# A four-layer backbone with mixtures of experts: experts' rows added to their tokens' sums in DRAM, where they were written apart and gathered twice

## The chip, the cores and the metric

The kernel runs on one core of a Trainium2 chip. The metric is the time of one execution in microseconds on the device, as the median of several runs. A core has five engines with a queue of instructions each, which they take in order: PE multiplies matrices (PEld loads its weights), DVE and ACT do elementwise work, POOL does elementwise work and issues the indirect transfers, SP issues most loads. The transfers of all queues run on the same 16 DMA engines of the core. An engine that needs another's result waits for a semaphore, and what stands behind it in its queue waits with it.

## The reference

Four layers work on 256 latent and 256 context tokens of 1024 values. Each applies a token mixer (attention, Mamba-2, mLSTM, latent attention) and then a mixture of 16 experts, of which every token uses two, with weights:

```python
xs = xs + g1x * yx
...
def hier_moe(h, w_rg, b_rg, w_re, b_re, w_gate, w_up, w_down):
    ...
    combine = jnp.sum(jax.nn.one_hot(eid, MOE_EXPERTS, dtype=jnp.float32) * w[..., None], axis=-2)
    out = jnp.zeros_like(h)
    for e in range(MOE_EXPERTS):
        act = jax.nn.silu(h @ w_gate[e]) * (h @ w_up[e])
        out = out + combine[..., e:e + 1] * (act @ w_down[e])
    return out
```

The experts' sum is multiplied by a gate (g2) and added to the stream x. In layers 0 to 2 this is done for all 512 tokens (four tiles of 128), in layer 3 for the 256 latent ones.

## The kernel before, in words

The program is written as a list of operations, and a scheduler sets their order on every engine once, when the program is built; a change in one place can so move instructions in others. Semaphores keep what depends on each other in order. A transfer's semaphore is one of eight that the transfers of a kind (those of SP and ACT together, those of POOL) take in turn, and a transfer that takes a semaphore again waits until the one before on it has landed.

`setup` makes constants. `layers` starts with eight loads of `w_mod` and the four tiles of x, whose first norms run on ACT (L287, `xn`).

In a layer's mixture, `route` makes for each expert a list of 128 slots (`gi`, one token's number per slot; empty slots have a number that is out of bounds). Behind it `slots_of` makes the row numbers `ri` by which the results will be found, and the slots' weights (`sw`). With 512 tokens, two experts each and 16 experts, half of the 2048 slots hold a token.

`experts` goes over the 16 experts. `gather` (L748, POOL) fetches an expert's rows from DRAM into one of four tiles `xg`; it skips the empty slots. PE transposes them (L761) and multiplies with the gate and up weights, each weight split into a high and a low half (`ehi` by ACT L742, `elo` by DVE L743). `down` multiplies with the third weight, and `rows` (L795 on DVE, L796 on ACT) writes the result, times the slots' weights, into one of three tiles `y`. `keep` (L800) then writes the tile, 512 KB, to the expert's own 128 rows of `yd` in DRAM. PE does the work of one expert's gate and up beside the down of the one before. SP loads weights into a ring of tiles (`wl`, `w`) that is four experts long. Expert 15 isn't written: its part goes to the tokens by matmuls with a selection matrix (`selT`).

`combine` runs between two layers. POOL issues eight indirect gathers (L931): four fetch each token's first row of `yd` into a tile w, and four add its second row to it on the way (`compute_op=add`). For each tile PE adds expert 15's part and this sum in PSUM (L942, L943, L946), DVE multiplies with g2 (L947) and adds to x (L952, a part of it on POOL L950). The next layer's norm follows tile by tile.

Of the kernel before, what the change touches and what calls it, by code (L numbers as in the profile page):

```python
# [7 lines left out]
F32 = mybir.dt.float32  # L8
F32R = mybir.dt.float32r
BF = mybir.dt.bfloat16  # L10
I32 = mybir.dt.int32
# [6 lines left out]
D = 1024  # L18
# [5 lines left out]
class Trunk:  # L24
# [8 lines left out]
    def setup(self):  # L33
# [52 lines left out]
        for c, pat, base, cm in ((0, [[0, 4], [0, 2]], 0, 1), (1, [[128, 4], [0, 2]], -4096, 0)):  # L86
# [3 lines left out]
        self.unit = self.const.tile([128, 16], F32, name="unit")  # L90
        nc.gpsimd.iota(self.unit, pattern=[[128, 16]], base=0, channel_multiplier=0,
                       allow_small_or_imprecise_dtypes=True)

# [338 lines left out]
    def route(self, pool, small, i, tiles, C, dense=False):  # L432
# [181 lines left out]
        with self.tc.issue_after(listed.ins):  # L614
            self.slots_of(S, a12, pk, ps, T, oh, weights, count)
        self.hd = hd

    def slots_of(self, S, a12, pk, ps, T, oh, weights, count):

        nc = self.nc  # L620

        nc.vector.tensor_mul(pk, a12, self.unit.unsqueeze(1).unsqueeze(1).to_broadcast([128, T, 2, 16]))
        rw = S("rw", [T * 2])
        nc.vector.tensor_reduce(rw, pk.rearrange("p t k e -> p (t k) e"), axis=AX.X, op=OP.add)
        nc.vector.tensor_add(rw, rw, ps)
        nc.vector.tensor_scalar(rw, rw, 128.0 * 15, None, op0=OP.min)
        self.ri = self.const.tile([128, 8], I32, name="ri")[:, :T * 2]
        nc.vector.tensor_copy(self.ri, rw)
# [99 lines left out]

    def experts(self, pool, i, tiles, yd, release):
# [5 lines left out]

        nc.gpsimd.dma_start(yd[15 * self.C:, :], xgs[-1][0:1, :])
# [62 lines left out]
        def keep(e, y, eng):  # L799
            return eng.dma_start(yd[e * 128:(e + 1) * 128, :], y)  # L800
# [5 lines left out]
        for e in range(15):  # L806
# [3 lines left out]
            if y:  # L810
                keep(e - 2, y, nc.gpsimd)
# [13 lines left out]
        keep(13, y, nc.gpsimd)  # L825
        y = rows(14, down(*late))
        keep(14, y, nc.scalar)
# [89 lines left out]
    def combine(self, pool, sT, yh, yl, yd, tiles):  # L917
# [3 lines left out]
        ys, end, first = {}, self.last_mm, None  # L921

        for ti, k in self.o["go"]:
            if not k and ti % 2 == 0:
                w = self.H.tile([128, 2048], F32, name="w", bufs=self.o["ring"])
                ys[ti], ys[ti + 1] = w[:, :D], w[:, D:]
            dst, add = ys[ti], dict(compute_op=OP.add) if k else {}
            if k and not ti and self.o["y0"]:
                dst, add = pool.tile([128, D], F32, name="y0"), {}
                first = dst  # L930
            last = nc.gpsimd.indirect_dma_start(  # L931
                out=dst, out_offset=None, in_=yd,
# [1125 lines left out]
```

## Time and profile before

| | |
|---|---|
| median of three runs | 2178.94 us (2167.51 to 2183.6) |
| profiled execution | 2178.66 us |
| its span | 2176.9 us, 30735 instructions |
| PE busy | 1935.9 us (89%) |
| DVE, ACT, POOL busy | 1493.3, 1037.2, 597.7 us |
| DMA | 467.22 MB, mean 215 GB/s |

Busy time counts the time in which an engine works. What it waits for stands in the lists of waits and in the chain that ended last, which goes back from the last instruction to what released each. The first layer's experts run from about 320 to 490 us, the second's and third's in the same way around 1080 and 1620 us. A row of the timeline has the start and the length in us, the engine, the line, out<-in, and in brackets how long the engine sat idle before and what ended that. "DMA to landing" is the time from an issue to the semaphore that says that all data has arrived, where the trace shows somebody who waits for it.

### The profile page before, as it was taken

How to read it: one execution, taken by the hardware profiler on the slowest of the kernel's cores; microseconds unless marked ns; L12 is line 12 of the kernel's file. 1: busy time of each engine (PE TensorE's matmuls, PEld its weight loads, DVE VectorE, ACT ScalarE, POOL GpSimd, SP SyncE). 2: the span in 40 equal slices, each digit the busy share in tenths (PEclk: the TensorE clock that was granted, in tenths of full speed). 3: DMA queues.
4: the chain of work that ended last, by engine and by line, in shares of the span. 5: the costliest groups of instructions: out<-in, count | busy, mean ns of one | idle time of the engine just before them, and what ended most of it. 6: DMA issues, size and time to landing. Idle time of an engine off the chain costs nothing.

```text
span 2176.9 us, 30735 instructions
## 1 busy us (share of the span) xinstructions
PE 1935.9 (89%) x11044; PEld 1440.9 (66%) x11044; DVE 1493.3 (69%) x2892; ACT 1037.2 (48%) x2054; POOL 597.7 (27%) x546
## 2 busy tenths in 40 slices
PE   5989979997988899896699969997879988998996
PEld 2965677765666676665577646886777765657542
DVE  3557567876798899888788755137768875586334
ACT  3447437764453443443377633226537764453111
POOL 2012241113564656564411121003331122001000
PEclk8989989998999999998799979999989998899998
DMA  9344758965635434444699547643649967707782
GB/s 340 134 154 158 260 178 329 396 226 154 197 111 159 139 135 142 143 162 155 222 335 397 205 130 227 223 181 117 227 175 352 406 209 235 286 15 282 280 307 101
DMA packets 176466, 467.22 MB, mean 215 GB/s; under 512 B 35065, under 2 KB 78177, under 8 KB 155824
## 3 DMA queue, kind: packets, MB, share of 16 engines
q1 hardware_dynamic: 152112, 396.01, 50.9%
q0 software_dynamic: 23488, 67.33, 9.6%
q8 instruction: 89, 1.46, 0.3%
q10 hardware_dynamic: 704, 1.82, 0.2%
q14 instruction: 73, 0.60, 0.1%
HBM read 446.44 MB, written 31.24 MB: 219 GB/s over the span
## 4 chain that ended last, share of the span: by engine, by line
PE 66%; DVE 19%; DMA 6%; ACT 3%; issue 3%; POOL 1%; SPq 0%; ACTq 0%; POOLq 0%; DVEq 0%
PE acc L201 11%; PE acc L202 11%; PE acc L203 11%; PE acc L779 3%; PE wm L225 3%; PE acc L872 3%; DVE M L1338 3%; DVE W L1344 2%; PE core L203 2%; PE core L201 2%; PE core L202 2%; PE tr L761 2%; DMA A<-acd 2%; PE tr L858 2%; PE core L1111 1%
## 5 line engine op out<-in xcount | busy, mean ns | idle before, releaser
L743 DVE TENSOR_TENSOR elo<-wl,ehi 128x1024 fp32r<-128x1024 f32 x156 | 187.1, 1220 | 22.2 <-ACT ehi L742 21.3
L742 ACT ACTIVATE ehi<-wl 128x1024 fp32r<-128x1024 f32 x156 | 161.4, 1055 | 54.3 <-PE acc L203 32.2
L748 POOL DMA_INDIRECT xg<-hd,gi x48 | 63.9, 1331 | 282.5 <-PE tr L761 227.5
L225 PE MATMUL wm<-w,cs 128*32 128x512 f32 x768 | 118.4, 634 | 20.3 <-DMA w<-in_w_mod_dram 20.2
L201 PE MATMUL acc<-hhi,wch 128*128 128x512 f32 (+1 forms) x336 | 132.7, 396 | 3.8 <-DVE zt L1311 2.7
L203 PE MATMUL acc<-split_hi,hlo 128*128 128x256 f32 x464 | 131.4, 285 | 0.2 <-DVE var L289 0.2
L202 PE MATMUL acc<-hlo,wch 128*128 128x512 f32 (+1 forms) x336 | 131.5, 392 | 0.0
L203 PE MATMUL acc<-hhi,wcl 128*128 128x512 f32 (+1 forms) x336 | 131.0, 391 | 0.0
L201 PE MATMUL acc<-split_hi,hhi 128*128 128x256 f32 x464 | 131.0, 287 | 0.0
L202 PE MATMUL acc<-split_lo,hhi 128*128 128x256 f32 x464 | 130.9, 284 | 0.0
L1263 POOL TENSOR_TENSOR wcl<-w,wch 128x512 fp32r<-128x512 f32 x76 | 109.5, 1454 | 65.9 <-ACT wch L1262 58.5
L201 PE MATMUL acc<-ehi,xTh 128*128 128x512 f32 x288 | 123.5, 429 | 2.7 <-ACT xTh L764 2.7
L202 PE MATMUL acc<-elo,xTh 128*128 128x512 f32 x288 | 118.0, 410 | 2.5 <-DVE elo L743 2.5
L203 PE MATMUL acc<-ehi,xTl 128*128 128x512 f32 x288 | 115.0, 399 | 0.0
L743 DVE TENSOR_TENSOR elo<-w,ehi 128x1024 fp32r<-128x1024 f32 x84 | 100.9, 1220 | 13.3 <-ACT ehi L742 13.3
L742 ACT ACTIVATE ehi<-w 128x1024 fp32r<-128x1024 f32 x84 | 87.0, 1052 | 27.0 <-PE acc L203 15.3
L201 PEld LDWEIGHTS acc<-split_hi,hhi 128*128 128x128 f32 x464 | 87.9, 191 | 10.2 <-issue 5.2
L376 POOL TENSOR_TENSOR x<-x,restmp 128x256 f32<-128x256 f32 (+1 forms) x46 | 48.5, 1054 | 165.4 <-DVE restmp L372 142.8
L1353 POOL TENSOR_TENSOR A<-A,CT 128x1024 f32<-128x1024 f32 x32 | 83.5, 2609 | 33.9 <-ACT A L1351 28.9
L196 DVE TENSOR_TENSOR split_lo<-w,split_hi 128x1024 fp32r<-128x1024 f32 x33 | 40.2, 1224 | 73.6 <-ACT split_hi L195 73.5
L203 PEld LDWEIGHTS acc<-split_hi,hlo 128*128 128x128 f32 x464 | 88.6, 191 | 2.7 <-DVE hhi L332 1.7
L202 PEld LDWEIGHTS acc<-split_lo,hhi 128*128 128x128 f32 x464 | 88.6, 191 | 1.5 <-issue 1.5
(613 smaller groups left out, 5674.8 us busy)
## 6 DMA issues: line engine op xcount, KB each, us to landing
w<-in_w_mod_dram SPq DMA_DIRECT2D x96, 1024.0 KB
wl<-in_moe_w_down_dram SPq DMA_DIRECT2D x47, 1024.0 KB
wl<-in_moe_w_gate_dram SPq DMA_DIRECT2D x82, 512.0 KB
wl<-in_moe_w_up_dram SPq DMA_DIRECT2D x82, 512.0 KB
w<-in_moe_w_gate_dram SPq DMA_DIRECT2D x46, 512.0 KB
w<-in_moe_w_up_dram SPq DMA_DIRECT2D x46, 512.0 KB
yd<-y POOLq DMA_DIRECT2D x42, 512.0 KB, 2.9
w<-in_ssm_w_in_dram SPq DMA_DIRECT2D x40, 512.0 KB
```

Of the source, the lines that this page charges most:

```text
L201: mm(ps, a[0], b[0], start=start, stop=False)
L202: mm(ps, a[0], b[1], start=False, stop=False)
L203: self.last_mm = mm(ps, a[1], b[0], start=False, stop=stop)
L225: nc.tensor.matmul(st["ps"][32 * g:32 * g + 32, :], self.cs[:, j, :], w[:, 512 * g:512 * g + 512], start=(j == 0), stop=(j == 7))
L742: nc.scalar.activation(hi, v, AF.Copy)
L743: nc.vector.tensor_sub(lo, v, hi)
L748: nc.gpsimd.indirect_dma_start(out=xgs[e % len(xgs)], out_offset=None, in_=self.hd, in_offset=bass.IndirectOffsetOnAxis(ap=self.gi[:, e:e ...
L779: nc.tensor.matmul(pg, x[2][:, jj, :], gu[1][:, :, 512 + 256 * jj:768 + 256 * jj], start=False, stop=(jj == 1))
L872: nc.tensor.matmul(pg[r, :], x[:, j, r], w[p][0][j // 4][:, :, j % 4 * 256:(j % 4 + 1) * 256], start=(j == 0), stop=(j == 7))
L1263: (eng or self.nc.gpsimd).tensor_sub(lo, v, hi)
L1338: nc.vector.scalar_tensor_tensor(M[:, h, c], CE[1][:, h, c], col(self.ac, 1, c, h), M[:, h, c], op0=OP.subtract, op1=OP.min)
L1353: nc.gpsimd.tensor_mul(Ah, Ah, CT.unsqueeze(1).to_broadcast([128, 2, 512]))
```

## The change

`yd` gets one row for each token (512) and 128 spare rows, and it is filled with zeros beforehand by five plain writes per layer on ACT's queue (`sums`). `keep` becomes an indirect scatter on POOL that adds the tile's rows to the rows of their tokens in DRAM (`compute_op=add`); slots without a token go to spare rows, one for each partition (`si`). `combine` loads one row per token with four plain loads on SP in place of the eight gathers on POOL. `ri` and the operations that made it go.

```diff
--- before.py
+++ after.py
@@ -87,9 +87,11 @@
             nc.gpsimd.iota(self.tokv[:, :, :, c], pattern=pat, base=base, channel_multiplier=cm,
                            allow_small_or_imprecise_dtypes=True)
 
-        self.unit = self.const.tile([128, 16], F32, name="unit")
-        nc.gpsimd.iota(self.unit, pattern=[[128, 16]], base=0, channel_multiplier=0,
+        self.spare = self.const.tile([128, 1], F32, name="spare")
+        nc.gpsimd.iota(self.spare, pattern=[[0, 1]], base=512, channel_multiplier=1,
                        allow_small_or_imprecise_dtypes=True)
+        self.zero = self.const.tile([128, 256], F32, name="zeros")
+        nc.gpsimd.memset(self.zero, 0.0)
 
         self.odd = self.const.tile([128, 8, 2], F32, name="odd")
         nc.gpsimd.iota(self.odd, pattern=[[0, 8], [64, 2]], base=0, channel_multiplier=0,
@@ -612,20 +614,15 @@
         self.gi = self.const.tile([128, 16], I32, name="gi")[:, :U]
         listed = nc.vector.tensor_copy(self.gi, xf)
         with self.tc.issue_after(listed.ins):
-            self.slots_of(S, a12, pk, ps, T, oh, weights, count)
+
+            self.si = self.const.tile([128, 16], I32, name="si")[:, :U]
+            nc.vector.tensor_scalar(self.si, xf, self.spare[:, 0:1], None, op0=OP.min)
+            self.slots_of(S, a12, ps, T, oh, weights, count)
         self.hd = hd
 
-    def slots_of(self, S, a12, pk, ps, T, oh, weights, count):
+    def slots_of(self, S, a12, ps, T, oh, weights, count):
 
         nc = self.nc
-
-        nc.vector.tensor_mul(pk, a12, self.unit.unsqueeze(1).unsqueeze(1).to_broadcast([128, T, 2, 16]))
-        rw = S("rw", [T * 2])
-        nc.vector.tensor_reduce(rw, pk.rearrange("p t k e -> p (t k) e"), axis=AX.X, op=OP.add)
-        nc.vector.tensor_add(rw, rw, ps)
-        nc.vector.tensor_scalar(rw, rw, 128.0 * 15, None, op0=OP.min)
-        self.ri = self.const.tile([128, 8], I32, name="ri")[:, :T * 2]
-        nc.vector.tensor_copy(self.ri, rw)
         weights()
         count()
 
@@ -726,14 +723,19 @@
         gu = [self.eload([v[:, h * D:(h + 1) * D] for v in (g, u)]).rearrange("p (k n) -> p k n", k=2) for h in range(2)]
         return gu, self.eload([self.I["moe_w_down"][i, e].rearrange("(p j) d -> p (j d)", j=2)])
 
+    def sums(self, i):
+
+        self.yd = self.DR.tile([5 * 128, D], F32, name=f"yd{i}")
+        for t in range(5):
+            self.nc.scalar.dma_start(self.yd[t * 128:(t + 1) * 128, :].rearrange("p (k n) -> p k n", n=256),
+                                     self.zero.unsqueeze(1).to_broadcast([128, 4, 256]))
+
     def experts(self, pool, i, tiles, yd, release):
         nc, T = self.nc, len(tiles)
         n = T * 128
         xgs = [pool.tile([128, D], F32, name=f"xg{k}") for k in range(self.o["ahead"])]
         for x in xgs:
             nc.gpsimd.memset(x, 0.0)
-
-        nc.gpsimd.dma_start(yd[15 * self.C:, :], xgs[-1][0:1, :])
 
         def chunk(v):
 
@@ -796,8 +798,11 @@
             nc.scalar.activation(y[:, 512:], py[1], AF.Copy, scale=w)
             return y
 
-        def keep(e, y, eng):
-            return eng.dma_start(yd[e * 128:(e + 1) * 128, :], y)
+        def keep(e, y):
+
+            nc.gpsimd.indirect_dma_start(
+                out=yd, out_offset=bass.IndirectOffsetOnAxis(ap=self.si[:, e:e + 1], axis=0), in_=y, in_offset=None,
+                bounds_check=n + 127, oob_is_err=True, compute_op=OP.add)
 
         for e in range(len(xgs)):
             gather(e)
@@ -808,7 +813,7 @@
             now = gate_up(e, x)
             gather(e + len(xgs))
             if y:
-                keep(e - 2, y, nc.gpsimd)
+                keep(e - 2, y)
             if late:
                 y = rows(e - 1, down(*late))
             x, late = nx, now
@@ -822,9 +827,9 @@
         sT = po.tile([128, 4, 128], F32R, name="selT")
         nc.scalar.activation(sT, pt.rearrange("p (t k) -> p t k", t=4), AF.Copy)
         sw = self.sw[:, 15:16]
-        keep(13, y, nc.gpsimd)
+        keep(13, y)
         y = rows(14, down(*late))
-        keep(14, y, nc.scalar)
+        keep(14, y)
         py = down(*gate_up(15, x))
         yh, yl = (po.tile([128, 2, 512], F32R, name="y" + k) for k in "hl")
         for nb in range(2):
@@ -918,20 +923,12 @@
 
         nc = self.nc
         g2 = self.mod_rows(pool, "g2", 2, 1)
-        ys, end, first = {}, self.last_mm, None
-
-        for ti, k in self.o["go"]:
-            if not k and ti % 2 == 0:
+        ys, end = {}, self.last_mm
+        for t in range(4):
+            if t % 2 == 0:
                 w = self.H.tile([128, 2048], F32, name="w", bufs=self.o["ring"])
-                ys[ti], ys[ti + 1] = w[:, :D], w[:, D:]
-            dst, add = ys[ti], dict(compute_op=OP.add) if k else {}
-            if k and not ti and self.o["y0"]:
-                dst, add = pool.tile([128, D], F32, name="y0"), {}
-                first = dst
-            last = nc.gpsimd.indirect_dma_start(
-                out=dst, out_offset=None, in_=yd,
-                in_offset=bass.IndirectOffsetOnAxis(ap=self.ri[:, 2 * ti + k:2 * ti + k + 1], axis=0),
-                bounds_check=yd.shape[0] - 1, oob_is_err=True, **add)
+                ys[t], ys[t + 1] = w[:, :D], w[:, D:]
+            nc.sync.dma_start(ys[t], yd[t * 128:(t + 1) * 128, :])
 
         def add(t, after=None):
             x, y, c = self.X[t], ys[t], self.o["cadd"][t]
@@ -941,13 +938,10 @@
                 with self.tc.issue_after((after or end).ins):
                     nc.tensor.matmul(ps, sT[:, t], yh[:, h], start=True, stop=False)
                 nc.tensor.matmul(ps, sT[:, t], yl[:, h], start=False, stop=False)
-                if not t and first is not None:
-                    nc.tensor.matmul(ps, self.ident, first[:, k], start=False, stop=False)
                 nc.tensor.matmul(ps, self.ident, y[:, k], start=False, stop=True)
                 nc.vector.tensor_mul(y[:, k], ps, g2[t // 2][:, k])
             if c:
-                with self.tc.issue_after(last.ins):
-                    nc.gpsimd.tensor_add(x[:, :c], x[:, :c], y[:, :c])
+                nc.gpsimd.tensor_add(x[:, :c], x[:, :c], y[:, :c])
             if c < D:
                 nc.vector.tensor_add(x[:, c:], x[:, c:], y[:, c:])
 
@@ -967,6 +961,8 @@
                 self.attn_proj(pb, w_in, kz, vr, qT)
             with self.tc.issue_after(self.last_pow.ins):
                 self.vectors()
+            if not self.dense:
+                self.sums(0)
             po = left.enter_context(self.pool("a_out"))
             with self.pool("a_soft") as pc:
                 hi, lo = self.attn_core(pc, po, kz, vr, qT)
@@ -1953,6 +1949,8 @@
                 self.fq.extend(self.mod_round(i, 1) + self.mod_round(i, 2))
                 if i < 3:
                     self.fq.extend(self.mod_round(i + 1, 0))
+                if 0 < i < 3 and not dense:
+                    self.sums(i)
                 mixers[i]()
                 if stop == f"xm{i}":
                     return self.dump()
@@ -1986,15 +1984,14 @@
                     listing.close()
                     with self.pool("moe_experts") as pool:
                         if i < 3:
-                            yd = self.DR.tile([15 * C + 1, D], F32, name=f"yd{i}")
                             last = ExitStack()
 
                             def release():
                                 keep.close()
                                 return last.enter_context(self.pool("moe_out", "right"))
 
-                            kept = self.experts(pool, i, tiles, yd, release)
-                            self.pending = self.combine(*kept, yd, tiles), last
+                            kept = self.experts(pool, i, tiles, self.yd, release)
+                            self.pending = self.combine(*kept, self.yd, tiles), last
                         else:
                             self.experts_select(pool, i, tiles)
                 picks.close()
```

The scheduler makes a new order of it. On ACT, the order at the start of the program before, the first row being the loads of a bias (`mod`) and `xn` the first norm:

```order
L49 ACTIVATE cth<-cc 128x16
L221 DMA mod_171<-in_b_mod_dram 4x512
L108 DMA vrows<-in_norm_g_dram 32x128
L221 DMA mod_1123<-in_b_mod_dram 4x512 x2
L287 ACTIVATE xn,ss<-x_69 128x1024
L287 ACTIVATE xn,ss<-x_70 128x1024
```

And now, with the three tensors `yd` of the three layers (lines are those of the changed kernel):

```order
L49 ACTIVATE cth<-cc 128x16
L223 DMA mod_173<-in_b_mod_dram 4x512
L110 DMA vrows<-in_norm_g_dram 32x128
L223 DMA mod_1125<-in_b_mod_dram 4x512 x2
L730 DMA yd_1337<-zeros 512x1x256 x5
L730 DMA yd_5224<-zeros 512x1x256 x5
L730 DMA yd_11717<-zeros 512x1x256 x5
L289 ACTIVATE xn,ss<-x_69 128x1024
L289 ACTIVATE xn,ss<-x_70 128x1024
```

All 15 fills of the three layers stand ahead of the first norm, though the diff places those of layers 1 and 2 in their layers. By the semaphores that the transfers take in turn, the eighth load of `w_mod` on SP now also waits for the ninth fill, and the first load of the attention's weights for the tenth.

On POOL, the end of the first layer's experts before, with the eight gathers of `combine` at L931 (`g` is the gate g2):

```order
L748 DMA xg_3571<-hd_3312,gi 128x1024
L800 DMA yd_3567<-y 128x1024 x5
L269 DMA g_5178<-md_2117 128x1024
L269 DMA g_5180<-md_2117 128x1024
L800 DMA yd_3567<-y 128x1024
L248 MEMSET mod_8432 64x512
L931 DMA w<-yd_3567,ri 128x1024 x8
L950 TENSOR_TENSOR x_70<-x_70,w 128x512
```

And now, where each scatter waits for a semaphore of POOL's transfers (DMASW), the one of the scatter before it among them:

```order
L750 DMA xg_3571<-hd_3320,gi 128x1024 [waits DMASW3_49,PE_49]
L803 DMA yd_1337<-y,si 640x1024 [waits DMASW0_49,DVE_49,Activation_49]
L750 DMA xg_3572<-hd_3320,gi 128x1024 [waits DMASW5_49,PE_49]
L750 DMA xg_3573<-hd_3320,gi 128x1024 [waits DMASW7_49,PE_49]
L803 DMA yd_1337<-y,si 640x1024 [waits DMASW3_49,DVE_49,Activation_49]
L803 DMA yd_1337<-y,si 640x1024 [waits DMASW6_49,DVE_49,Activation_49]
L803 DMA yd_1337<-y,si 640x1024 [waits DMASW7_49,DVE_49,Activation_49]
L803 DMA yd_1337<-y,si 640x1024 [waits DMASW0_49,DMASW1_49,DVE_49,Activation_49]
```

The gathers at the end have gone, the plain writes, which waited for no other, have become a row of scatters of which each waits for the one before, and nine of them instead of six stand behind the last gather of inputs. On SP, the end of the experts' weights and the next mixer's first loads before:

```order
L714 DMA wl<-in_moe_w_down_dram 128x2048
L714 DMA wl<-in_moe_w_gate_dram 128x1024
L714 DMA wl<-in_moe_w_up_dram 128x1024
L714 DMA wl<-in_moe_w_down_dram 128x2048
L1249 DMA w<-in_ssm_w_in_dram 128x8x128 x2
L176 DMA w<-in_ssm_w_in_dram 128x4x64 x2
```

And now:

```order
L711 DMA wl<-in_moe_w_gate_dram 128x1024
L711 DMA wl<-in_moe_w_up_dram 128x1024
L711 DMA wl<-in_moe_w_down_dram 128x2048 x2
L931 DMA w<-yd_1337 128x1024 x4
L1245 DMA w<-in_ssm_w_in_dram 128x8x128 x2
L178 DMA w<-in_ssm_w_in_dram 128x4x64 x2
```

The four loads of the sums stand ahead of the next mixer's weights, and they wait for the last scatter.

## Rows read from the trace of the kernel before

**Rows 1.** The page, part 1: busy time of PE, share, instructions.

```profile
PE 1935.9 (89%) x11044; PEld 1440.9 (66%) x11044; DVE 1493.3 (69%) x2892; ACT 1037.2 (48%) x2054; POOL 597.7 (27%) x546
```

**Rows 2.** The chain that ended last, 0 to 110 us: start, us, what.

```profile
6.70 11.67 DMA x<-in_ctx_dram
...
18.43 13.73 DMA w<-in_w_mod_dram
...
33.88 8.71 DMA w<-in_w_mod_dram
```

**Rows 3.** Windows of the start: busy us by engine, PEclk, DMA share, GB/s.

```profile
30.00:35.00 5.00, 3.63 (x19) 0.57 (x12) 0.69 (x1) 0.10 (x1) 0.00 (x0) 0.67 1.02 384
...
40.00:45.00 5.00, 4.87 (x39) 2.85 (x38) 4.98 (x9) 5.00 (x10) 0.26 (x1) 1.00 0.60 194
```

**Rows 4.** Timeline of ACT at the start: start, us, what, idle before.

```profile
18.39 1.06 ACT L287 ACTIVATE xn<-x 128x1024 f32<-128x1024 f32 x1 [13.67 <-DMA x<-in_ctx_dram]
```

**Rows 5.** Windows of the first expert stage (columns as in rows 3).

```profile
360.00:380.00 20.00, 20.00 (x90) 15.24 (x89) 17.43 (x23) 14.91 (x23) 3.97 (x4) 1.00 1.01 392
...
460.00:480.00 20.00, 18.91 (x86) 14.46 (x85) 15.40 (x22) 14.33 (x20) 2.12 (x4) 1.00 0.33 106
```

**Rows 6.** Timeline of POOL, first expert stage and its end.

```profile
349.98 0.60 POOL L800 DMA_DIRECT2D yd<-y  x1
...
377.44 1.42 POOL L748 DMA_INDIRECT xg<-hd,gi  x1 [7.74 <-PE tr L761]
...
387.17 1.42 POOL L748 DMA_INDIRECT xg<-hd,gi  x1 [7.74 <-PE tr L761]
...
473.66 0.54 POOL L800 DMA_DIRECT2D yd<-y  x1 [6.08 <-ACT y L796]
...
483.67 1.09 POOL L931 DMA_INDIRECT w<-yd,ri  x1 [1.30 <-DMA yd<-y]
```

**Rows 7.** Line 748, the gathers of experts' inputs, 360 to 430 us.

```profile
L748 POOL DMA_INDIRECT xg<-hd,gi x7: 1417/1418/1418, 367.7 to 426.1; - x7
...
DMA to landing us min/median/max: 9.0/9.1/9.1
```

**Rows 8.** Line 800, the writes of experts' results, whole run.

```profile
L800 POOL DMA_DIRECT2D yd<-y x42: 531/570/600, 350.0 to 1774.8; - x42
...
DMA to landing us min/median/max: 2.9/2.9/2.9
```

**Rows 9.** Line 931: four adding gathers; the last line for all 24.

```profile
L931 POOL DMA_INDIRECT w<-yd,ri x4: 1543/1569/1620, 489.0 to 494.8; - x4
...
DMA to landing us min/median/max: 9.4/9.4/9.4
...
DMA to landing us min/median/max: 5.7/9.4/9.9
```

**Rows 10.** Windows between layers 0 and 1 (columns as in rows 3).

```profile
486.00:492.00 6.00, 4.53 (x19) 2.92 (x17) 3.84 (x6) 3.45 (x6) 4.66 (x5) 1.00 0.90 316
...
493.00:503.00 10.00, 5.53 (x10) 2.44 (x11) 2.44 (x3) 0.00 (x0) 3.04 (x2) 0.66 1.05 204
```

**Rows 11.** Timeline of PE between layers 0 and 1.

```profile
490.01 0.39 PE L942 MATMUL core<-yh,selT 128*128 128x512 f32 x1
...
490.24 0.39 PE L943 MATMUL core<-yl,selT 128*128 128x512 f32 x1
...
497.48 2.07 PE L946 MATMUL acc<-w,ident 128*128 128x512 f32 x2 [6.85 <-DMA w<-yd,ri]
```

**Rows 12.** A window within PE's wait (columns as in rows 3).

```profile
494.00:497.00 3.00, 0.00 (x0) 0.00 (x0) 0.00 (x0) 0.00 (x0) 2.04 (x2) 0.52 1.08 205
```

**Rows 13.** The chain that ended last, 440 to 530 us.

```profile
480.25 2.63 DMA yd<-y
...
489.01 8.42 DMA w<-yd,ri
```

**Rows 14.** Timeline of SP's queue at the end of the stage.

```profile
450.37 2.80 SPq L1249 DMA_DIRECT2D w<-in_ssm_w_in_dram  x2
```

## The prediction

> **What bounds the kernel now.** I read the page first: PE is busy for 89% of the span [rows 1], so time is won or lost only where PE waits or where it is fed more slowly. The changed operations lie at two places where another thing than PE is the limit, and in one where two limits are nearly level.
>
> At the start, the chain that ended last consists of transfers alone up to about 42 us: loads of x from 6.70, of `w_mod` from 18.43 and again from 33.88 [rows 3]. The DMA share is 1.02 at 384 GB/s there, and falls to 0.60 only after 40 us [rows 2]. ACT's first norm waits 13.67 us for x [rows 4]; it has slack, the transfers have none.
>
> Between two layers, PE has done its own part at 490.24 + 0.39 and waits 6.85 us, to 497.48, for the sums [rows 11]. The chain runs from the last expert's write (480.25, landed after 2.63) over a gather issued at 489.01 that takes 8.42 us [rows 13]. The reader is to see that the eight gathers are what ends last here: the first is issued at 483.67 [rows 6], and the engines then move 204 GB/s at a share of 1.05, where plain rows go at 316 at a share of 0.90 [rows 10]. In the wait PE's clock is granted at 0.52 [rows 12].
>
> In the experts' stage PE is busy for 20.00 of 20 us, but the DMA share is 1.01 at 392 GB/s as well [rows 5]. Two limits are level there: SP runs ahead of PE by its ring of weights, and the engines have room only at the end, where the share is 0.33. An expert takes 9.73 us (377.44 to 387.17 on POOL) [rows 6].
>
> **The change part by part.** That it does what it says is seen in the order: 15 scatters and four loads per layer, no gather of results.
>
> *Zero fills.* 15 fills of 0.524 MB are 7.9 MB. At the start's 384 GB/s [rows 2] that is 20 us of transfer. The fills share DMA engines with SP's loads, and the eighth load of `w_mod` waits for the ninth fill, so that at least nine of them, 12 us, get in between the loads which the chain is made of. Bounds: 0, if the rest slid behind 40 us and the first nine in gaps that rows 2 doesn't show, and 26, if their pieces of 1 KB (the order's 512x1x256) move a third slower than weights do. I take 17, since some of the last six will find the room after 40 us. ACT's norms stand behind all 15 issues, but what follows them needs the eighth load of `w_mod` too.
>
> *The scatters' own price.* No row shows an adding transfer into DRAM. The four adding gathers moved 204 GB/s for about 10 us [rows 10], 2.6 us for each 512 KB, twice the 1.3 us of plain rows at 392 GB/s [rows 5]. From issue to landing the adding gathers took 9.4 us (5.7 to 9.9 over all) [rows 9], behind others in the same queue; a plain write of the same tile landed after 2.9 us on idle engines [rows 8]. So with idle engines a scatter takes between 4.2 (2.9, plus 1.3 for adding) and 9.4; I take 7.5. In the saturated stage the nearest row is the gather of inputs, which is indirect too: 9.0 to 9.1 us [rows 7], though it moves only half of its rows, 0.7 us of transfer against 2.6. So a scatter there takes from 9.1 to 11.1 us; I take 10.2, and 0.3 more until the next is issued, since POOL has 1.5 us of issue for an adding one [rows 9] where a plain write has 0.57 [rows 8].
>
> *The chain of scatters.* Each waits for the one before, and POOL's gathers of inputs queue behind that wait. Those are needed several experts later, and cost nothing until the chain is two experts late. The chain may begin where the first write of `y` stands, 349.98, and the last gathers now begin at 483.67 [rows 6]: 133.7 us for 15, or 8.9 us each. At 10.5 it can't hold that. The stage gets 15 x 1.3 = 20 us of additional transfer, which fills the room after 460, so I count 12 scatters at 10.5 (to 476) and three at 7.5: the last lands at 498.5, where the gathers before began at 483.67.
>
> *The end of the layer.* The four loads of sums are plain and wait for that landing. At 2.9 us [rows 8] the first is there at 501.4, and the others follow at 1.3 each. Before, PE went on at 497.48 [rows 11]. That is 4 us lost per layer; the last tile comes no later than before, but ACT's norms take the tiles one by one from the first. Three layers lose 12 us. The first loads of the next mixer's weights were issued at 450.37 [rows 14] and now stand behind the sums; they'd land before 510 and be hidden by the norms. If the norms were no cover, they would cost about 5 us in one layer.
>
> *Moved matmuls.* The order on PE is the same to about the tenth expert; then the downs of experts 9 to 11 stand up to some 20 matmuls later, at 0.23 us from one to the next [rows 11] less than 5 us. The late chain covers that. It costs up to 4 us per layer if the chain were in time. *Lists:* six small operations on DVE go and one comes, under 1 us per layer beside the first gathers; nothing.
>
> *Weights.* With 11 us of transfer per expert against 9.73 of PE, the loads fall behind by 20 us in all, against a ring of four experts, 39 us. Nothing, or up to 3 us at the last experts.
>
> *Sum.* The profiled execution took 2178.66 us, which is the median. 2178.7 + 17 + 12 = 2208 us.
>
> **A rule weighed.** The gathers in the saturated stage take 9.0 to 9.1 us where the plain write takes 2.9 [rows 7, 8]. The Trainium skill, "DMA: Bandwidth & Descriptors", section "Anatomy of one DMA — SWDGE (gpsimd) path", gives a POOL-issued transfer about 2.0 us and its bytes at 436 GB/s, an estimate of 3.2 us for 512 KB. By that rule a scatter is far below 8.9 us, the chain is in time, and the first rival below comes true. The plain write agrees with it (2.9), the gathers in the stage don't (9.1), so the trace bears it out for idle engines alone.
>
> **The rivals.**
>
> *The chain keeps pace* (not slower). It decides at 8.9 us per scatter, with all else as above. Then the last scatter is issued when its tile is ready, 480.25 [rows 13], lands 7.5 later at 487.8, and the first sum is there at 490.7, when PE has just ended its part. 6.7 us gained per layer, 20 in all: 2178.7 + 17 - 20 = 2176. For it: 10.5 is an estimate between 9.1 and 11.4, and a scatter not behind a gather may be quicker. Against it: the saturated share of 1.01 leaves nothing for 1.3 us more per expert.
>
> *The chain keeps pace and the fills are hidden* (faster). If the fills found gaps, 2159, and some 2 us less per layer where PE's clock no longer falls in a wait: 2153. Against it: the share of 1.02 in rows 2.
>
> *The chain is far behind.* If reading rows back from DRAM before adding lengthens a scatter to 14 us, 12 of them end at 518. `y` has three tiles, so PE would stop for them near the stage's end; loads then slow too, and the engines have room again. I put 25 to 30 us on a layer: 2178.7 + 17 + 85 = 2281. For it: no row has an adding write into DRAM.
>
> **How the numbers follow.** A measurement of this kernel can tell about 1% from no change, some 22 us: 2157 to 2201. The forecast (a chain that lags, 2190 to 2255) has 0.48, the chain in time 0.27, in time with hidden fills 0.12, far behind 0.13. Faster by over 1%: 0.12, the third. Within 1%: the second's 0.25 and 0.10 of the forecast, in all 0.35. Slower: 0.53. The range of 2163 to 2264 leaves out the far case above and most of the hidden fills below.
>
> **What would show it.** In the profile after, the first norm on ACT should begin near 40 us instead of 18.39, and PE's transposes of it some 17 us later than before. From one scatter's issue to the next on POOL there should be 10 to 11 us in the stage, ended by the transfer of the scatter before, and 7 to 8 at the end. The DMA share should stay near 1.0 to about 475, and the first matmul on a loaded sum (L941) should come about 20 us later than in rows 11, 4 of them in the first layer and the rest from the start. The prediction is wrong in its main step if the scatters wait for `y` rather than for each other, and in its second if ACT's first norm begins before 25 us.

## The result, and the profile after

The changed kernel takes 2243.5 us (median of six runs, 2237.7 to 2248.1) against 2178.8 us: 1.030 times as long, 95% interval 1.027 to 1.032, some 65 us slower. The profiled execution has a span of 2242.8 us against 2176.9.

Three events per layer divide the span: the first gather of inputs on POOL, PE's first matmul on a loaded sum (L941; L946 before), and the next layer's first gather. Their times, read from the timelines, make this table; a stage runs from the gather to the matmul, a mixer from there to the next layer's gather.

| us | start | stages of layers 0, 1, 2 | mixer 1 | mixer 2 | end, from layer 2's matmul on a sum |
|---|---|---|---|---|---|
| before | 316.8 | 180.7, 181.0, 179.7 | 580.3 | 360.4 | 378.0 |
| after | 338.0 | 188.4, 190.8, 188.7 | 584.3 | 365.4 | 387.3 |
| longer by | 21.2 | 26.5 | 4.0 | 5.0 | 9.3 |

**The start.** The chain that ended last in the kernel after, 0 to 110 us, now has the fills where loads stood [rows 2]:

```profile
11.61 17.71 DMA yd<-zeros
...
31.81 9.82 DMA yd<-zeros
41.70 8.40 DMA w<-in_w_mod_dram
```

ACT's timeline shows its queue held by the issues until the last fill is in the queue, and the first norm behind it, at 44.01 where it was at 18.39 [rows 4]:

```profile
10.18 33.78 ACTq L730 DMA_DIRECT2D yd<-zeros  x15
44.01 1.06 ACT L289 ACTIVATE xn<-x 128x1024 f32<-128x1024 f32 x1 [39.29 <-DMA yd<-zeros]
```

**The stage.** Line 803 holds the scatters, over the whole run: 10.0 us to landing, 6.1 where the engines are free (writes took 2.9 [rows 8]).

```profile
L803 POOL DMA_INDIRECT yd<-y,si x45: 1552/1589/2587, 369.0 to 1845.4; - x45
...
DMA to landing us min/median/max: 6.1/10.0/10.6
```

Windows of the first stage of the kernel after (columns as in rows 3); those from 360 and from 460 us answer to [rows 5]:

```profile
360.00:380.00 20.00, 20.00 (x93) 15.54 (x92) 16.66 (x24) 15.11 (x24) 4.90 (x3) 1.00 0.97 324
...
440.00:460.00 20.00, 19.33 (x91) 14.67 (x90) 16.86 (x28) 14.82 (x24) 4.86 (x3) 1.00 1.00 355
460.00:480.00 20.00, 16.60 (x74) 12.49 (x75) 13.56 (x18) 10.68 (x16) 1.71 (x2) 1.00 0.89 302
480.00:500.00 20.00, 18.72 (x77) 13.54 (x76) 16.87 (x22) 15.41 (x22) 5.71 (x3) 1.00 0.46 72
```

The DMA stays full up to 460 (share 1.00) and nearly so to 480 (0.89); from 480 on, at 0.46 and 72 GB/s, the scatters have it almost to themselves. POOL's timeline in that stage (before: [rows 6]):

```profile
414.07 1.59 POOL L803 DMA_INDIRECT yd<-y,si  x1 [6.72 <-DVE xTl L767]
415.96 1.11 POOL L750 DMA_INDIRECT xg<-hd,gi  x1 [0.31 <-issue]
425.37 1.38 POOL L750 DMA_INDIRECT xg<-hd,gi  x1 [8.30 <-PE tr L763]
427.05 2.59 POOL L803 DMA_INDIRECT yd<-y,si  x1 [0.31 <-issue]
435.09 1.44 POOL L750 DMA_INDIRECT xg<-hd,gi  x1 [5.45 <-PE tr L763]
444.82 1.82 POOL L750 DMA_INDIRECT xg<-hd,gi  x1 [8.29 <-DVE elo L745]
446.94 1.62 POOL L803 DMA_INDIRECT yd<-y,si  x1 [0.31 <-issue]
458.57 1.58 POOL L803 DMA_INDIRECT yd<-y,si  x1 [10.01 <-DVE xTl L767]
...
509.75 1.67 POOL L803 DMA_INDIRECT yd<-y,si  x1 [4.09 <-DMA yd<-y,si]
516.68 1.58 POOL L803 DMA_INDIRECT yd<-y,si  x1 [5.26 <-DMA yd<-y,si]
517.72 1.08 POOL L250 MEMSET mod<- 64x512 f32 x1
```

From scatter to scatter it is 11 to 12 us in the stage, but 13.0 (414.07 to 427.05) and 19.9 (427.05 to 446.94) where two gathers stand between two scatters. A gather waits until PE has transposed the tile that it overwrites, and the scatter behind it waits along, though its rows and the landing before it are long there. The engines that the profile names beside 6.72 or 10.01 us had been done; those scatters wait for the one before. At the end a scatter follows the other every 7 us.

**Between the layers.** ACT and PE at the end of the first stage, one fence each:

```profile
518.83 0.52 ACTq L252 DMA_DIRECT2D mod<-in_norm_g_dram  x1
519.39 0.53 ACTq L223 DMA_DIRECT2D mod<-in_b_mod_dram  x1
519.96 0.38 ACT L696 ACTIVATE actTh<-tr 128x256 fp32r<-128x256 f32 x1 [13.06 <-issue]
```

```profile
520.40 0.80 PE L203 MATMUL core<-ehi,actTh 128*128 128x512 f32 x1 [12.02 <-ACT actTh L696]
...
526.37 1.12 PE L941 MATMUL acc<-w,ident 128*128 128x512 f32 x2
```

PE stops for 12 us before its last down projection. It waits for `actTh`, which stands on ACT behind a load into `mod`; that load waits for the memset of `mod` (517.72), which stands on POOL behind the last scatter. Below, the next mixer's weights on SP, and DVE:

```profile
523.09 1.75 SPq L931 DMA_DIRECT2D w<-yd  x4
524.93 1.79 SPq L1245 DMA_DIRECT2D w<-in_ssm_w_in_dram  x2
```

```profile
527.53 0.69 DVE L942 TENSOR_TENSOR w<-acc,g 128x512 f32<-128x512 f32 x1 [1.12 <-PE acc L941]
528.87 0.69 DVE L942 TENSOR_TENSOR w<-acc,g 128x512 f32<-128x512 f32 x1 [0.65 <-PE acc L941]
533.91 1.29 DVE L1259 TENSOR_TENSOR wcl<-w,wch 128x512 fp32r<-128x512 f32 x2 [4.35 <-ACT wch L1258]
535.12 0.68 DVE L942 TENSOR_TENSOR w<-core,g 128x512 f32<-128x512 f32 x1
```

The mixer's first weights, issued at 450.37 before [rows 14], are issued at 524.93, behind the sums. DVE works in order, and the split of these weights (L1259) stands in its queue among the operations of the combination, so that the third product with g2 comes only at 535.12.

**The last layer.** But for layer 2's combination at its start, nothing of the change runs there, yet it takes 9 us more. The 64 matmuls of `w_mod` in it (L227; each fp32 matmul has two records) took 18.1 us of PE before, 26.2 after. Windows of that line alone, from layer 2's first matmul on a sum on, in the kernel after and in e2 below (length, PE, PEld, PEclk, DMA share, GB/s):

```profile
1855.50:2242.80 387.30, 26.19 (x128) 3.79 (x128) 0.95 0.59 213
```

```profile
1837.70:2216.20 378.50, 18.91 (x128) 2.88 (x128) 0.94 0.60 219
```

PE's timeline of the kernel after shows why:

```profile
1926.71 1.07 PE L227 MATMUL wm<-w,cs 128*32 128x512 f32 x8
...
1938.52 1.04 PE L227 MATMUL wm<-w,cs 128*32 128x512 f32 x2
...
1940.40 1.05 PE L227 MATMUL wm<-w,cs 128*32 128x512 f32 x2
...
1942.29 1.04 PE L227 MATMUL wm<-w,cs 128*32 128x512 f32 x2
```

Each such matmul uses 32 columns of the array, and four for different columns stood one behind the other before. The scheduler, run again on the changed program, put some of them apart with other matmuls in between, and one alone (x2) takes 1.04 us where four together (x8) take 1.07. The Trainium skill, "TensorEngine Tiling (Array Packing)", section "Tiling Modes", says that different tiles of the array can work in parallel; the trace agrees (1.07 us for four, 1.04 for one).

### The profile page after: what moved, and what is told of

The parts are those of the page before. It is cut to its first block, busy times and chain, and to the rows that moved or that the text cites. A ratio compares the mean times of both kernels' runs of the same rounds, so it can differ in the third digit from the quotient of the medians.

```text
span 2242.8 us, 30738 instructions
## 1 busy us (share of the span) xinstructions
PE 1950.4 (87%) x11044; PEld 1445.7 (64%) x11044; DVE 1491.7 (67%) x2880; ACT 1038.1 (46%) x2054; POOL 620.6 (28%) x523
## 4 chain that ended last, share of the span: by engine, by line
PE 60%; DVE 18%; DMA 13%; issue 3%; ACT 3%; POOL 1%; SPq 0%; ACTq 0%; POOLq 0%; DVEq 0%
PE acc L203 10%; PE acc L204 10%; PE acc L205 9%; DMA yd<-y,si 4%; PE wm L227 3%; PE acc L877 3%; DVE M L1334 3%; PE acc L781 3%; DVE W L1340 2%; DMA A<-acd 2%; DMA w<-in_w_mod_dram 2%; PE core L205 2%; PE core L203 2%; PE core L204 2%; PE tr L763 1%
## 5 line engine op out<-in xcount | busy, mean ns | idle before, releaser
L745 DVE TENSOR_TENSOR elo<-wl,ehi 128x1024 fp32r<-128x1024 f32 x156 | 187.2, 1220 | 28.1 <-ACT ehi L744 26.5
L227 PE MATMUL wm<-w,cs 128*32 128x512 f32 x768 | 127.1, 649 | 44.1 <-DMA w<-in_w_mod_dram 44.1
L803 POOL DMA_INDIRECT yd<-y,si x45 | 78.6, 1746 | 219.8 <-DVE elo L745 44.9
L1259 POOL TENSOR_TENSOR wcl<-w,wch 128x512 fp32r<-128x512 f32 x76 | 109.7, 1456 | 64.9 <-ACT wch L1258 56.7
L203 PE MATMUL core<-ehi,actTh 128*128 128x512 f32 x192 | 80.2, 421 | 35.8 <-ACT actTh L696 35.7
L744 ACT ACTIVATE ehi<-w 128x1024 fp32r<-128x1024 f32 x84 | 87.0, 1053 | 37.5 <-PE core L205 14.1
```

The source lines that it names most:

```text
L203: mm(ps, a[0], b[0], start=start, stop=False)
L227: nc.tensor.matmul(st["ps"][32 * g:32 * g + 32, :], self.cs[:, j, :], w[:, 512 * g:512 * g + 512], start=(j == 0), stop=(j == 7))
L744: nc.scalar.activation(hi, v, AF.Copy)
L745: nc.vector.tensor_sub(lo, v, hi)
L803: nc.gpsimd.indirect_dma_start(out=yd, out_offset=bass.IndirectOffsetOnAxis(ap=self.si[:, e:e + 1], axis=0), in_=y, in_offset=None, bounds ...
L1259: (eng or self.nc.gpsimd).tensor_sub(lo, v, hi)
```

## The experiments

All times are medians; "loss" is against the runs of the kernel before on the same chip (2176.5 to 2180.3 us). The loss of the changed kernel is 64.7 us.

**e1_fills_alone**

```diff
 (before)
+        yz = self.DR.tile([5 * 128, D], F32, name=f"yz{i}")
+        for t in range(5):
+            self.nc.scalar.dma_start(yz[t * 128:(t + 1) * 128, :]..., self.zero...)
```

> The kernel before plus the fifteen zero fills alone, written into tensors that nothing reads; its combination stays. Theory: the fills push the first loads of w_mod back by their own transfer time and nothing hides it, so 2179 + 20 to 22 = 2199 to 2201 us, with the first norm's work about 21 us later and all later stages as before. Rival: the 21 us that the changed kernel loses ahead of its first expert gather come from the scheduler's new order, and the fills run beside other work: within 5 us of before.

2197.0 us, ratio 1.009 (1.005 to 1.012), loss 20.4: the theory's. The first norm begins at 44.44 and the first gather at 337.6, 20.8 later than before the change. That the whole comes out at the same figure is partly luck: mixer 1 takes 570.7 us, 9.6 less than before, and the end 389.4, 11.4 more, with 26.2 us for the last layer's `w_mod` matmuls. So with the combination of before, but another order, the last layer is as slow as in the changed kernel, and it is the scheduler's order that costs there.

**e2_fills_late**

```diff
-            self.nc.scalar.dma_start(self.yd[t * 128:(t + 1) * 128, :]..., self.zero...)
+            self.zq.append((yd, t))
...
+            done = nc.scalar.activation(hh, pv, AF.Copy)
+            self.clear(done)
```

> The changed kernel with its fifteen fills issued one by one behind the sixteen output activations of the attention core (172 to 260 us, DMA share 0.43 to 0.51 there). Theory: the start is as before the change, and the attention core has room for 7.9 MB: 2243.5 - 21 = 2222 us, first expert gather near 317 us instead of 338. Rival: the fills only collide with the expert weights that are loaded ahead in that stretch, and the gathers start about 10 us later than that: 2233 us.

2214.0 us, ratio 1.016 (1.012 to 1.019), loss 37.5. Fills done behind attention's outputs cost nothing: the first gather comes at 317.3, and the DMA share from 172 to 262 us rises from 0.50 in the changed kernel to 0.74. 27 us are gained and not 21: the end is back at 378.5 us, 8.8 shorter, with the `w_mod` matmuls in fours; the mixers are 3.7 us shorter together, and the stages 6.5 longer.

**e3_mod_dve**

```diff
-                nc.gpsimd.memset(n2, 0.0)
+                nc.vector.memset(n2, 0.0)
```

> The changed kernel with the memset of mod (line 250) on VectorE instead of GpSimd, where it stood behind the last scatter and held, by way of two loads on ScalarE's queue, the last expert's activations and PE's last down projection for 12 us per layer. Theory: PE's wait lies beside the end of the chain of scatters, and the sums can't be loaded sooner: 0 to 2 us a layer, 2238 to 2243.5 us. Rival: the three waits of PE (35.7 us in all) are what the combination costs: 2243.5 - 33 = about 2210 us.

2239.7 us, ratio 1.030 (1.026 to 1.035), loss 63.2. PE's timeline in e3: it ends its own part at 510.1, and then waits for the sums instead.

```profile
509.73 0.40 PE L940 MATMUL acc<-yl,selT 128*128 128x512 f32 x1
522.72 1.22 PE L941 MATMUL acc<-w,ident 128*128 128x512 f32 x1 [12.60 <-DMA w<-yd]
```

The most conspicuous wait of the profile after, 35.7 us of PE in all, was beside the chain of scatters, and taking it away gives next to nothing: the stages are 190.1, 191.8 and 186.9 us, in sum 0.9 longer.

**e4_sums_pool**

```diff
-            nc.sync.dma_start(ys[t], yd[t * 128:(t + 1) * 128, :])
+            nc.gpsimd.dma_start(ys[t], yd[t * 128:(t + 1) * 128, :])
```

> The changed kernel with the four loads of sums issued by GpSimd, right behind its last scatter, instead of SyncE, whose queue then goes on to the next mixer's weights without waiting. Theory: the 18 us that are lost between the first matmul on a sum and the next layer's first gather (4.0, 5.0 and 9.2 us) are mostly weights that stood behind the sums: 2243.5 - 12 = 2231 us (2226 to 2236). Rival: these loads aren't late enough to matter, and loads from GpSimd take longer to land: 2243 to 2248 us.

2220.9 us, ratio 1.019 (1.016 to 1.023), loss 44.4: 20 us gained, more than expected, but not all of it by this cause. Mixer 1 is 10.9 us shorter and the end 13.5, of which 5 are the `w_mod` matmuls (21.0 us here), while the stages are 10 longer. These parts are of one execution of 2230.0 us, 9 above the median; e8 and e12 are the cleaner pair, and there the stages don't differ by the queue of these loads.

**e5_pin**

```diff
-            gather(e + len(xgs))
-            if y:
-                keep(e - 2, y)
+            with ExitStack() as behind:
+                if y:
+                    behind.enter_context(self.tc.issue_after(keep(e - 2, y).ins))
+                gather(e + len(xgs))
```

> The changed kernel with each scatter ahead of the gather of the same turn on GpSimd's queue (in the changed kernel six turns put one or two gathers, which wait for PE's transposes, ahead of the scatter: spaces of 13 and 19.9 us between scatters in the stage). The scheduler here also keeps the last layer's mod matmuls in groups of four, which alone should give 8 us. Theory: the chain of scatters sets the end of the stage and these spaces lengthen it, so the last scatter lands 3 to 5 us sooner in each of three layers: 2243.5 - 8 - 12 = 2223 us. Rival: the chain's last five links, 7 us each behind the late experts' rows, set the end alone: 2243.5 - 8 = 2235 us, with the stages 188 to 191 us long as they are.

2209.1 us, ratio 1.014 (1.012 to 1.016), loss 30.9. POOL's timeline in e5 shows scatter, gather, scatter, at 10.7 to 12.0 us:

```profile
407.27 2.62 POOL L803 DMA_INDIRECT yd<-y,si  x1 [7.44 <-ACT ehi L744]
410.19 1.04 POOL L750 DMA_INDIRECT xg<-hd,gi  x1 [0.31 <-PE core L205]
419.23 1.59 POOL L803 DMA_INDIRECT yd<-y,si  x1 [7.99 <-DVE xTl L767]
421.12 1.34 POOL L750 DMA_INDIRECT xg<-hd,gi  x1 [0.31 <-PE tr L763]
429.97 1.59 POOL L803 DMA_INDIRECT yd<-y,si  x1 [7.51 <-ACT ehi L744]
431.86 1.46 POOL L750 DMA_INDIRECT xg<-hd,gi  x1 [0.31 <-issue]
440.88 2.23 POOL L803 DMA_INDIRECT yd<-y,si  x1 [7.55 <-DVE elo L745]
```

The stages are 185.6, 185.3 and 183.3 us: 13.7 us gained in them (12 expected), 5.4 at the end. The other 16 us of the gain lie in the start (331.4) and the mixers (580.1, 359.7), which the edit doesn't touch. The 6.6 at the start go with PE's granted clock, as the last section shows: e7, with the same order of instructions as the changed kernel, has its first gather at 331.8 too. The 10 us in the mixers stay unexplained.

**e6_two_sums**

```diff
-                out=yd, out_offset=...
+                out=yd[e % 2], out_offset=...
...
+            nc.sync.dma_start(y2[t], yd[1][t * 128:(t + 1) * 128, :])
...
+                nc.tensor.matmul(ps, self.ident, y2[t][:, k], start=False, stop=False)
```

> The kernel with late fills (e2, 2214 us) and two tensors of sums: even experts add into one, odd ones into the other, so that a scatter waits for the one before the last; thirty fills, eight loads and eight more identity matmuls on PE. Theory: that each scatter waits for the landing of the one before is what lengthens the stages (191.5, 193.0 and 189.9 us there, 180 before the change); with two chains of some 20 us a link none waits, and the stages are 181 to 184 us: 2214 - 27 = 2187 us (2183 to 2195, some of it lost to the second set of fills). Rival: the adding's traffic and not its order is what costs, DMA being full in the stage: 2210 to 2218 us.

2177.2 us, ratio 1.000 (0.998 to 1.001), no loss; 37 us less than e2. The last line of the scatters' source in e6:

```profile
DMA to landing us min/median/max: 6.2/10.8/12.1
```

A scatter takes no less time to land than before, the traffic is the same or more, and the stages are 177.5, 177.0 and 169.7 us. They end sooner than with gathers partly because a stage ends here with the matmul on the odd sum, which doesn't wait for expert 14. From one layer's first gather to the next's it takes 756.5 and 538.0 us, against 778.0 and 552.5 in e2 and 761.0 and 541.4 before the change, so the chain's loss is gone and a little more. What cost was that the scatters waited for each other, not their bytes.

**e7_plain**

```diff
-                bounds_check=n + 127, oob_is_err=True, compute_op=OP.add)
+                bounds_check=n + 127, oob_is_err=True)
```

> The changed kernel with scatters that write instead of adding (the sums then hold the last expert's row of each token alone, and not the sum); every engine's instructions stand in the same order, and each scatter still waits for the one before. Theory: the adding doubles the time that a scatter holds the DMA engines and its landing; plain ones land in 5 to 6 us in the stage (10.0 now) and 3 to 4 at its end (6.1 now), the chain keeps up with the experts, and each stage is 6 to 8 us shorter: 2243.5 - 21 = 2222 us. Rival: the landing is the price of an indirect write and of the full DMA, whatever it does to the rows there: landing 9 to 10 us and 2238 to 2243 us.

2206.0 us, ratio 1.012 (1.009 to 1.015), loss 27.9. The two lines of the source view in e7 that answer to those of the kernel after:

```profile
L803 POOL DMA_INDIRECT yd<-y,si x45: 973/1060/2054, 365.2 to 1811.6; - x45
...
DMA to landing us min/median/max: 3.3/7.8/10.4
```

Adding costs 2.8 us of landing on free engines (6.1 to 3.3), 2.2 us at the median, and 0.5 us of issue on POOL. In the stage the plain scatter was expected to land in 5 to 6 us, and took 7.8 at the median. The stages are 180.0, 177.7 and 176.5 us, 33.7 us less than in the changed kernel, more than the 21 expected: though POOL's spaces of 17 and 20 us are still there, the late links follow at 4 to 5 us instead of 7 and catch up, until the last two wait for `y`. The Trainium skill, "DMA: Bandwidth & Descriptors", section "Anatomy of one DMA — SWDGE (gpsimd) path", gives for a transfer from POOL an estimate of 3.2 us for 512 KB. On free engines the plain scatter meets it, 3.3 us, and the adding one, 6.1, doesn't.

**e8_all** and **e12_all_sync**. e8 joins the edits of e2, e3, e4 and e5; e12 is e8 without that of e4.

> Late fills (e2), the memset of mod on VectorE (e3), the loads of sums on GpSimd (e4) and scatters ahead of gathers (e5) together. Theory: 2243.5 - 21 (start) - 8 (the last layer's mod matmuls in fours) - 11 (the ssm mixer's weights not behind the sums) - 9 (the chain without the spaces) + 6 (loads from GpSimd land later) = 2200 us, which leaves the stages at about 188 us, 7 longer than before the change, and the kernel slower than before by 1%. Rival: the gains lie one behind the other in the same waits and don't add up: 2210 to 2215 us.

> As e8 (2190 us), with the loads of sums on SyncE again; the last layer's mod matmuls are grouped as in e8, and PE's order differs in few places, which they did not in e4. Theory: of the 22 us that e4 gained, 8 were the mod matmuls and some 10 the next mixers' weights, which no longer stood behind the sums: 2190 + 10 = 2200 us, most of it in the ssm mixer (577 us from the first matmul on a sum to the next gather in e8, 584 to 586 in the kernels with these loads on SyncE). Rival: the loads on GpSimd land later and give back what the freed queue brings: 2188 to 2192 us.

e8: 2190.3 us, ratio 1.005 (1.003 to 1.007), loss 12.1; the gains do add up, further than expected. e12: 2205.1 us, ratio 1.012 (1.010 to 1.014), loss 27.4. In e12, the sums' loads on SP cost 15 us, and not, as expected, most of it in mixer 1: that is 5.7 us longer than in e8 and the end 9.2, while the sum of the stages is the same (554.8 and 555.2). SP in e12, then DVE in e12 and in e8, behind the first layer's experts:

```profile
499.45 1.75 SPq L940 DMA_DIRECT2D w<-yd  x4
501.30 1.70 SPq L1256 DMA_DIRECT2D w<-in_ssm_w_in_dram  x2
```

```profile
510.51 1.29 DVE L1270 TENSOR_TENSOR wcl<-w,wch 128x512 fp32r<-128x512 f32 x2 [16.71 <-ACT wch L1269]
511.72 0.69 DVE L951 TENSOR_TENSOR w<-acc,g 128x512 f32<-128x512 f32 x1
```

```profile
504.47 0.69 DVE L951 TENSOR_TENSOR w<-acc,g 128x512 f32<-128x512 f32 x1 [8.96 <-PE acc L950]
505.08 1.28 DVE L1270 TENSOR_TENSOR wcl<-w,wch 128x512 fp32r<-128x512 f32 x2
```

In e8 the weights are on their way from 453.8 on, and their split doesn't hold up the first product with g2.

**e9_two_sums_spread, e10_two_sums_pin, e11_two_sums_sync**. The edits stand in their expectations.

> Two sums (e6, 2177 us), with its fills spread over the projections and the core of attention and twenty-four of them (the spare rows, which nothing reads, stay uncleared), the memset of mod on VectorE and the loads of the even sums on GpSimd. Theory: the first gather comes at 317 us again (322.5 in e6), the ssm mixer's weights wait less and the last layer's mod matmuls are in fours: 2177 - 5 - 4 - 5 = 2163 us, faster than both kernels. Rival: the chain was the only loss left, and what these edits free is hidden behind other waits: 2174 to 2180 us.

> As e9, with thirty fills and each scatter ahead of the gather of its turn on GpSimd. Theory: with two chains no scatter is waited for, so the order on GpSimd gives nothing: the time of e9 within 6 us, 2163 to 2169. Rival: the order still held up the landing of the last scatters, and it gains what it gained with one chain (3 to 5 us a layer): 2150 to 2155 us.

> As e9, with thirty fills and the loads of the even sums on SyncE again. Theory: with the last scatter landing earlier the next mixer's weights wait less for it, so the queue of these loads matters less than it did in e4: 3 to 5 us slower than e9, about 2167 us. Rival: the loads from GpSimd, which land later, cost what the freed queue gives: the same time as e9.

e9: 2167.2 us, ratio 0.996 (0.994 to 0.997), 13 us faster than before the change, between theory and rival. The start didn't come back: its first gather is at 323.1 us, not 317. e10: 2174.0, 0.998 (0.997 to 0.999). e11: 2175.9, 0.999 (0.997 to 1.001). e9 has stages of 175.9, 177.3 and 169.2 us. With two chains the order on POOL gives nothing, as expected (the stages of e10 are no shorter: 176.0, 177.6, 176.3), but the time of e10 is 5 us above the theory's. Where its 7 us beyond e9 lie can't be told, as its profiled execution is 10.6 us above its median. e11's 9 us fit the theory in sign, more than in size. Both have thirty fills where e9 has twenty-four, and they are within 2 us of each other; the six fills are a rival that no run separates.

## Why the prediction was right and wrong

The direction was right. The size was not: +29 us were forecast, +65 measured. Three steps failed. The chain's step passed over the turns on POOL: 12 us were forecast for the three stages, 26.5 measured. The step on the end of the layer put the next mixer's weights at nothing: 10 to 15 us. The step on moved matmuls put them at nothing: 8 us in the last layer. The two terms that carried the sum, fills and chain by itself, were near what the runs show. (Of the sources cited for the start, rows 2 and rows 3 are exchanged: the chain stands in rows 2, the share of 1.02 in rows 3.)

The loss of 64.7 us splits into differences of losses: 20.4 in e1, its start being the fills; 6.8 more up to e2; 10.1 from e2 to e12, the turns on POOL and the memset; 15.3 from e12 to e8, the queue of the sums' loads; 12.1 left in e8, the chain itself. Each has an uncertainty of some 5 us, since every edit also moves the scheduler's order.

- *Zero fills, 17 us:* 20.4 to 21.2, by e1's time and by the first gather of the changed kernel. The mechanism is shown (e1, e2). None of the last six found room: the DMA share stays at 1.02 to 1.09 up to 60 us.
- *The scatters' price, 10.2 and 7.5 us:* 10.0 and 6.1. Right in the stage, 1.4 too high behind it.
- *The chain, 12 us in three layers:* with the scatters at their turn it is 12.1 us of time in e8; the stages are 13.8 us longer than before there, 13.4 in e12. That the chain is the cause is shown by its absence in e6 and its shortening in e7. In the changed kernel the stages lost 26.5, since the step saw only one half of POOL's queue; e5, which changes the turns alone, gives 13.7 of them back. "POOL's gathers of inputs queue behind that wait" is true, but the scatters queue behind the gathers' wait for PE as well. The changed order had two gathers ahead of a scatter at two places in every layer, and could be read before the run.
- *"They'd land before 510 and be hidden by the norms":* put at nothing, and 15 us are lost from e8 to e12: 5.7 us in mixer 1 and 9.2 in the end (2.3 of them `w_mod` matmuls, 22.24 against 19.95 us), 0.4 in mixer 2. Against the kernel before it may be less: in the changed kernel mixers and end are 18.3 us longer, 8.1 of them `w_mod` matmuls, which leaves 10. The prediction's own bound without the cover, 5 us in one layer, fits mixer 1. DVE's queue holds the splits of these weights among the operations of the combination, so the norms are what waits, and can't be the cover. In the last layer DVE shows the same: 7.9 us from the first to the second product with g2 in e12, 2.2 in e8.
- *Moved matmuls, nothing:* right for the downs that were named: e3 shows PE waiting behind them. Wrong in where it looked: the moves that cost were in the last layer, 1500 us behind the first scatter: 8.1 us of PE (26.2 against 18.1).
- *Rivals.* That e6 takes 2177 us, the figure of the chain in time (2176), is luck: e6 has its fills hidden too, the case for which 2153 to 2159 was said. From gather to gather its first two layers gain 4.5 and 3.4 us on the kernel before, not 6.7. The far chain's mechanism, PE stopped by `y`, didn't come: `y` for expert 14 was written by 504.2 us, and its scatter issued at 516.68; PE did stop, for `mod`, and it cost nothing (e3).
- *What would show it:* the first norm (44.01) and PE's transposes (53.80 where 35.13 stood) came as said; so did 7 to 8 us between the last scatters and the full DMA. The spacing in the stage didn't (13.0 and 19.9 at two places), nor the first matmul on a sum, 28.9 us later where 20 was said.

## What to carry to other kernels

A wait that is added to an instruction is also a wait for all that stands behind it on its queue, and for the engines those serve: before costing it at nothing, read in the order what stands behind it on that engine, and what stands ahead of it. Operations that add into one tensor follow each other at their landing time; two tensors in turn halve the chain for a few loads and fills more, and here took away the 37 us that were left once the fills were hidden (e2 to e6); the gain of 0.4% in e9 has other edits in it. When a scheduler orders the whole program, compare the order in stages that the change doesn't touch, and measure with the combination of before and the new order (as e1 did by chance) before explaining what they lose.

Whether the chain could be shortened by leaving out the wait, no run here shows. The Trainium skill, "DMA: Bandwidth & Descriptors", section "Two DMAs through the same engine are not ordered", reports that of two read-modify-writes of one row right behind each other the second mostly read stale data.

## What was not expected of the hardware

- An adding scatter of 512 KB lands 2.8 us later than a plain one on free engines (6.1, 3.3) but only 2.2 us later at the median of the stage (10.0, 7.8): the full DMA adds 3.9 us to the one and 4.5 to the other.
- Four matmuls of 32 columns side by side take 1.07 us and one alone 1.04: a scheduler that puts them apart cost 8 us of PE for 64 of them.
- Two executions with the same order of instructions up to there (the changed kernel and e7) reached the first gather at 338.0 and 331.8 us. What differs is PE's granted clock. In both PE waits in the attention, busy for 14.1 of the 20 us from 140 to 160, and the clock falls to 0.50, the lower of its two levels (1.2 of 2.4 GHz). It is back at 1.00 by 165 us in e7, and by 180 in the changed kernel. Windows of the kernel after and of e7 below (columns as in rows 3):

```profile
160.00:170.00 10.00, 10.00 (x46) 8.94 (x44) 4.37 (x18) 3.23 (x13) 2.14 (x2) 0.50 0.16 52
```

```profile
160.00:170.00 10.00, 10.00 (x77) 7.76 (x79) 6.77 (x26) 5.72 (x23) 2.26 (x3) 0.92 0.43 135
```

  Of the six profiled executions with the fills at the start, the three with 0.50 in this window (the changed kernel, e1, e4) have the first gather at 337.0 to 338.0 us, and the three with 0.92 to 0.96 (e3, e5, e7) at 331.4 to 332.7. These 6 us belong to no edit. The kernel before has the long stretch too (0.50 from 140 to 150), so that the 21.2 us at the start compare like with like.
